# The head of a gated-linear-attention stage moved among the last projection products, its branch moved behind it

## The chip, the cores and the metric

One core of a Trainium2 chip runs the kernel. The metric is device time in microseconds: the median of three runs is 2146.17 us (2144.84 to 2146.43).

## What is computed

A decoder trunk with two layers takes 2048 prompt rows and 64 sample rows of width 1024. The first layer (pooling and differential attention) is not touched here. The second layer is gated linear attention:

```python
q, k, v, g = split(x @ w_in); log_a = log_sigmoid((x @ w_ga) @ w_gb + b_g) / 16
o, s_end = gla_chunked(q, k, v, log_a, s0)          # 4 heads, key 128, value 256
o = rms_norm(o, norm_w) * silu(g)
y = layer_norm(alpha * x + o @ w_out)
```

The recurrence works on tiles of 128 rows: o of a tile is q times the state S before it plus a causal product inside the tile, and S is carried on with the gates' decay.

## The kernel before

`project_odd` (L1426) makes q, k, gates, v and silu(g) times the norm weights. It is a Strassen-like scheme: `fast` (L184) runs seven products m in the order 1, 2, 6, 7, 4, 5, 3, each of four parts j, and yields after each part of a product's second half. Results go to DRAM: q1, k1, cb1 (gates), v1, sg1 (silu rows). Weights of a product are loaded in units of 512 KB into a ring of two raw buffers (`O.raw`, tiles wr, gs, gmi) by SP's queue, split into a hi part (L40 on ACT or L44 on DVE) and a lo part (L45 on DVE), and kept in four places (tiles wk); every fp32 product is three matmuls of such parts (L51 to L53).

In `Odd.run` (L1348) the last projection (row half 1, the gates' columns) is consumed part by part. At part (7, 3) it opens the Gla object and from then on takes one step of `early` (L1381) after each part: loads for tiles 0 and 1, the inside products of both (`inside`, L1759), splits of tile 0, and output weight 0. Then the projection's pools are closed, output weights 1 and 2 are loaded, the register `r` is read (whether the decay is too steep for the short form), and a branch runs `G.run(True)` or, in the other arm, `weights_inside` and `G.run(False)`.

`run_in` (L1816) is the tile loop. It opens its pools over the memory that the projection's tiles had (a tile waits until the old ones in its memory are no longer read), loads the sg1 rows of tiles 0 and 1 and the norm weights, and for i = 0..15 weaves `out(i - 1)` (transposes, 48 products with the output weights, LayerNorm) with `fill(i)`: `mix(i)` (o in PSUM tile go, then the state products gsp, then S, Sh, Sl), `scale(i)` (the RMS norm and gates, tile gm), three steps of the samples, and `prepare(i + 1)`. In `fill(0)` stand also output weights 3 to 7, through the same two raw buffers (tiles gs). The tile that holds o is two PSUM banks with one buffer.

The order on an engine is not the text's alone: the framework (`schedule_with_timeline_sim=True`, L2390; "the planner" below) takes the instructions that are ready by its own estimates, and the older one first. What stands in a branch is planned on its own.

Of the kernel before, what the change touches and what calls it, by code (L numbers as in the profile page):

```python
# [1312 lines left out]
class Odd:  # L1313
# [34 lines left out]
    def run(self):  # L1348
        tc, d, ctx = self.tc, self.d, self.ctx
        nc = tc.nc  # L1350
        self.steep = self.pool(ctx, "p1s", 1).tile([1, 32], I32, name="steep")[:, 0:1]
        cst = self.pool(self.p1, "p1c", 1)
        tu = self.pool(self.p1, "p1t", 4)
        last = project_odd(tc, d, self, cst, tu)
# [12 lines left out]
        self.fill_banks.close()  # L1367
        for k in range(1, 3):
            self.out_weights(G, k, self.place)
        gw = places(self.pool(ctx, "gw", 3, side="right"))  # L1370
        for k in range(3, 8):
            G.w.append((gw if k > 4 else self.place)(300 + k))
        G.buf["s"] = [self.raw.tile([128, 1024], F32, tag="raw", name=f"gs_{i}") for i in range(2)]
        r = nc.values_load(self.steep[0:1, 0:1], min_val=0, max_val=1)
        with tc.If(r < 1) as c:
            G.run(True)
        with c.Else():
# [3 lines left out]
    def early(self, G, gw):  # L1381
# [3 lines left out]

        for i in range(2):
            G.load(i, G.first + ("v1",))
        yield
        for i in range(2):
            for _ in G.inside(i, 1, True, bank):  # L1390
                yield
            if i:
                G.two("v", G.R[0], "v1", "act")
            else:
                G.two("a", G.R[0], "att", "dve")
                self.out_weights(G, 0, places(gw))
# [29 lines left out]
def project_odd(tc, d, O, cst, tu):  # L1426
# [5 lines left out]
    left = [Room(O.pool(O.p1, f"p1l{i}", 1)) for i in range(3)]  # L1432
# [280 lines left out]
class Gla:  # L1713
# [3 lines left out]
    def __init__(self, tc, d, ident, raw, gl):  # L1717
# [8 lines left out]
        for key, n, w in (("a", 1, 512), ("k", 2, 512), ("v", 1, 1024)):  # L1726
            for part in "hl":
                self.buf[key + part] = [gl.tile([128, w], F32R, name=f"g{key}{part}_{i}") for i in range(n)]
        self.buf["dec"] = [gl.tile([128, 2, 4, 8], F32, name=f"gdec{i}") for i in range(2)]
# [14 lines left out]
    def load(self, i, keys):  # L1744
# [3 lines left out]
        for key in keys:  # L1748
# [6 lines left out]
            else:  # L1755
                r[key] = self.get(key) if key == "v1" else self.io.tile([128, 1024], F32, tag=key, name=f"g{key}{i}")[:n]
# [52 lines left out]
    def run(self, fast):  # L1809

        R, buf = {i: dict(r) for i, r in self.R.items()}, {k: list(b) for k, b in self.buf.items()}
        with ExitStack() as ctx:
            self.run_in(ctx, fast)
        self.R, self.buf = R, buf

    def run_in(self, ctx, fast):  # L1816
# [8 lines left out]
        io = self.io = pool("gio", 2)  # L1825
        wk = pool("gwk", 1)
        sk = pool("gsk", 1)
        sm = pool("gsm", 4)
# [3 lines left out]
        pz = pool("gpz", 2, space=PSUM)  # L1832

        def bank(name):
            return pt.tile([128, 512], F32, tag="pt", name=name)

        first = self.first if fast else self.first + ("att",)
        S = wk.tile([128, 4, 256], F32, name="S")
        Sh = wk.tile([128, 4, 256], F32R, name="Sh")
        Sl = wk.tile([128, 4, 256], F32R, name="Sl")  # L1840
        for i in range(2):
            load(i, ("sg1",) if fast else ("att", "sg1"))
        g = wk.tile([128, 1024], F32, name="lng1")
        b = wk.tile([128, 1024], F32, name="lnb1")
        nc.sync.dma_start(g, d["ln_g"][1])
# [567 lines left out]
```

## Time and profile before

| | |
|---|---|
| median of three runs | 2146.17 us |
| the profiled execution | 2143.98 us |
| its span, first to last instruction | 2142.2 us |
| mean granted TensorE clock, of full speed | 0.978 |
| busy: PE, DVE, ACT, POOL | 94%, 69%, 48%, 41% |

PE is TensorE, DVE VectorE, ACT ScalarE, POOL GpSimd, SPq the queue of SyncE that issues most loads. In a table by stretch each engine has its busy time and its number of instructions; PEclk is the share of full speed that was granted (1.00 is 2.4 GHz, 0.50 is 1.2 GHz). In a list of instructions the first number is the start, the second the duration; in brackets stands how long the engine had been idle before it, and what ended that. Ends of matmuls are modelled.

### The profile page before, as it was taken

The page shows a single profiled execution, that of the slowest core. Times are in us where ns is not written, and L with a number is a line of the kernel's source. Part 1 is how long each engine was busy: PE and PEld are TensorE (multiplying, and loading weights), DVE is VectorE, ACT ScalarE, POOL GpSimd, SP SyncE. Part 2 cuts the span into 40 slices and gives each one's busy share as a digit, 9 for nine tenths or more (in the row PEclk, how much of TensorE's full clock was granted, in tenths as well). Part 3 has the DMA queues.
Part 4 walks back from the last instruction along what each step waited for, and adds up shares of the span by engine and source line. Part 5 has one row for each costly group of instructions (what it writes and reads, how often), then busy time and mean ns, then how long its engine had stood idle before and what let it go on. Part 6 is the DMA issues. An engine that isn't in the chain of part 4 may idle for free.

```text
span 2142.2 us, 31455 instructions
## 1 busy us (share of the span) xinstructions
PE 2007.9 (94%) x10769; PEld 1639.6 (77%) x10769; DVE 1479.3 (69%) x2762; ACT 1024.7 (48%) x1922; POOL 878.4 (41%) x1167
## 2 busy tenths in 40 slices
PE   8989998998999999889898899999999897999997
PEld 7868786877788777677786688788887676787786
DVE  7697657565876676798767776667634557777784
ACT  4144433345633455664555533445428665455552
POOL 2345444323754532666543513222111122555654
PEclk9999999999999999999999999999999998999999
DMA  8877777447964698553322558666543457455532
GB/s 289 268 247 237 254 258 233 166 110 199 285 202 150 172 293 290 157 188 121 111 70 74 175 176 301 224 215 216 167 149 126 152 180 260 148 183 179 166 107 76
DMA packets 210395, 405.64 MB, mean 189 GB/s; under 512 B 29122, under 2 KB 106306, under 8 KB 210226
## 3 DMA queue, kind: packets, MB, share of 16 engines
q1 hardware_dynamic: 139490, 231.43, 35.7%
q0 software_dynamic: 50240, 158.48, 20.9%
q10 hardware_dynamic: 20496, 13.63, 2.1%
q8 instruction: 87, 1.43, 0.3%
q14 instruction: 82, 0.67, 0.1%
HBM read 275.90 MB, written 127.55 MB: 188 GB/s over the span
## 4 chain that ended last, share of the span: by engine, by line
PE 68%; DVE 10%; DMA 9%; ACT 5%; issue 5%; POOL 2%; SPq 1%; ACTq 0%; POOLq 0%; DVEq 0%
PE f L51 11%; PE f L52 11%; PE f L53 11%; PE po L1061 3%; PE gz L53 3%; PE gz L51 3%; PE gz L52 3%; PE sc L1016 2%; PE sc L1017 2%; PE tp L1068 2%; ACT e L1036 2%; DVE nm L1021 2%; DMA pt<-pn 1%; PE zp L51 1%; PE zp L53 1%
## 5 line engine op out<-in xcount | busy, mean ns | idle before, releaser
L1036 ACT ACTIVATE e<-sc,nm 128x896 f32<-128x896 f32 (+11 forms) x192 | 164.8, 864 | 127.1 <-DVE nm L1034 89.4
L1021 DVE TENSOR_REDUCE nm<-sc 128x1 f32<-128x768 f32 (+7 forms) x160 | 156.7, 991 | 26.1 <-PE sc L1017 15.4
L45 DVE TENSOR_TENSOR wk<-wr,wk 128x1024 fp32r<-128x1024 f32 x80 | 98.3, 1230 | 97.8 <-ACT wk L40 97.6
L45 DVE TENSOR_TENSOR wl<-wr,wh 128x1024 fp32r<-128x1024 f32 (+1 forms) x90 | 108.8, 1211 | 82.1 <-ACT wh L40 72.4
L1016 PE MATMUL sc<-kst,qh 128*128 128x512 f32 (+9 forms) x352 | 134.5, 385 | 30.2 <-ACT e L1036 28.8
L1061 PE MATMUL po<-vt,aT 128*128 128x128 f32 x1088 | 154.4, 282 | 2.5 <-ACT aT L1073 2.2
L40 ACT ACTIVATE wh<-wr 128x1024 fp32r<-128x1024 f32 (+1 forms) x85 | 88.0, 1038 | 139.6 <-PE f L52 71.7
L1061 PEld LDWEIGHTS po<-vt,aT 128*128 128x128 f32 x1088 | 139.2, 196 | 9.3 <-ACT aT L1073 2.5
L40 ACT ACTIVATE wk<-wr 128x1024 fp32r<-128x1024 f32 x77 | 81.3, 1058 | 129.5 <-PE f L53 94.0
L1073 ACT ACTIVATE aT<-tp 128x512 f32<-128x512 f32 (+3 forms) x160 | 85.4, 534 | 98.0 <-PE tp L1068 97.5
L1017 PE MATMUL sc<-kst,ql 128*128 128x512 f32 (+9 forms) x352 | 122.2, 350 | 0.0
L1016 PEld LDWEIGHTS sc<-kst,qh 128*128 128x128 f32 x352 | 68.5, 195 | 50.2 <-ACT e L1036 41.0
L1068 PE MATMUL tp<-ident,e 128*128 128x128 f32 x544 | 91.2, 282 | 11.6 <-ACT aT L1073 10.2
L1045 DVE SCALAR_TENSOR_TENSOR e<-e,c,e 128x128 f32<-128x128 f32 (+15 forms) x64 | 96.1, 1502 | 1.4
L1068 PEld LDWEIGHTS tp<-ident,e 128*128 128x128 f32 x544 | 63.9, 144 | 25.8 <-ACT aT L1073 15.2
L1017 PEld LDWEIGHTS sc<-kst,ql 128*128 128x128 f32 x352 | 68.7, 195 | 4.0 <-issue 0.2
L1039 DVE TENSOR_TENSOR s<-s 128x1 f32<-128x1 f32 x64 | 21.2, 331 | 70.5 <-ACT e L1036 70.1
L1092 POOL TENSOR_SCALAR s1q<-s 128x1 f32<-128x1 f32 x64 | 16.9, 265 | 102.4 <-DVE s L1039 78.2
L53 PE MATMUL op<-wh,ol 128*128 128x512 f32 x128 | 52.7, 411 | 5.1 <-DVE ol L1232 5.1
L51 PE MATMUL op<-wh,oh 128*128 128x512 f32 x128 | 53.4, 417 | 1.2 <-ACT oh L1231 1.1
L52 PE MATMUL gz<-wl,gmh 128*128 128x512 f32 x128 | 51.5, 402 | 1.1 <-DVE wl L45 1.1
L51 PE MATMUL zp<-wh,zh 128*128 128x512 f32 x128 | 52.2, 410 | 0.0
(872 smaller groups left out, 6665.0 us busy)
## 6 DMA issues: line engine op xcount, KB each, us to landing
wr<-in_w_q SPq DMA_DIRECT2D x75, 512.0 KB, 4.9
wr<-pt SPq DMA_DIRECT2D x40, 512.0 KB, 7.5
wr<-rt SPq DMA_DIRECT2D x40, 512.0 KB, 4.4
sk<-in_cachek SPq DMA_DIRECT2D x64, 256.0 KB, 3.6
sv<-in_cachev SPq DMA_DIRECT2D x64, 256.0 KB, 4.7
pt<-pn POOLq DMA_DIRECT2D x32, 256.0 KB, 7.1
qr<-q SPq DMA_DIRECT2D x64, 128.0 KB, 4.4
kr<-k SPq DMA_DIRECT2D x32, 256.0 KB, 4.5
```

Source lines behind the costliest of these rows:

```text
L40: h = nc.scalar.activation(hi, raw, AF.Copy)
L45: return h, (lo_eng or nc.vector).tensor_tensor(out=lo, in0=raw, in1=hi, op=ALU.subtract)
L51: nc.tensor.matmul(ps, lh(k), rh(k), start=(first and k == 0), stop=False, **kw)
L52: nc.tensor.matmul(ps, lh(k), rl(k), start=False, stop=False, **kw)
L53: nc.tensor.matmul(ps, ll(k), rh(k), start=False, stop=(last and k == n - 1), **kw)
L1016: nc.tensor.matmul(o, qh[:, c, qs], kst[:, ks], start=True, stop=False)
L1017: nc.tensor.matmul(o, ql[:, c, qs], kst[:, ks], start=False, stop=k < npc - 1)
L1021: nc.vector.tensor_reduce(out=nm[:, c, i:i + 1], in_=p[:, :, :w], op=ALU.max, axis=AX.XY, negate=True)
L1036: nc.scalar.activation(o, p, AF.Exp, bias=nm[:, m, 0:1], accum_out=s[:, m, i if npc > 1 else 0:][:, :1])
L1045: nc.vector.scalar_tensor_tensor(out=es[0][:, :nk], in0=es[1][:, :nk], scalar=c2, in1=es[0][:, :nk], op0=ALU.mult, op1=ALU.add)
L1061: nc.tensor.matmul(po, s[:, 128 * j:128 * j + 128], vt[:, k0 + j, :], start=(k0 + j == 0), stop=(k0 + j == n - 1))
L1068: nc.tensor.transpose(p[:, 128 * j:128 * j + 128], a[:, 128 * (k0 + j):128 * (k0 + j) + 128], self.ident)
```

## The change

- `S`, `Sh`, `Sl` become tiles of the Gla object, in memory of their own, and not of the tile loop's pool.
- `mix` becomes a method, and o is written to two tiles of one bank each; tile 0's `mix` runs in `early`, with its o in the projection's PSUM pool.
- `early` has twelve steps and not seven: output weights 0 and 1 after both tiles' inside products, into the room of a22; tile 0's mix after part (5, 3); the splits of tile 1 and the loads of tile 2; weights 2 and 3 into the room of s1. Weights 4 to 7 go into the places wk, in `fill(0)`. All hi parts are on ACT, the lo parts of weights 3, 5 and 7 on POOL.
- The tile loop's pools are put in another order over the projection's memory: the sg1 rows lie where the tiles t were, y0 where u was, the split q and gm where v was. In `fill(0)` the loads of the samples and of the norm weights come after weights 4 to 7.
- `G.run(True)` runs without a condition, and only the other form stands in a branch, behind it.

```diff
@@ Odd.run
-                early = self.early(G, self.pool(ctx, "gw0", 1, side="right"))
+                early = self.early(G)
             elif early:
                 next(early, None)
-        for _ in early:
-            pass
+        r = nc.values_load(self.steep[0:1, 0:1], min_val=0, max_val=1)
         self.p1.close()
         self.fill_banks.close()
-        for k in range(1, 3):
-            self.out_weights(G, k, self.place)
...
-        with tc.If(r < 1) as c:
-            G.run(True)
-        with c.Else():
+        G.run(True, early)
+
+        with tc.If(r > 0):
             weights_inside(tc, d)
             G.run(False)
@@ early
+            if i == 0:
+                G.two("v", R[0], "v1", "act")
+                G.two("a", R[0], "att", "act")
+            yield
+        self.out_weights(G, 0, room(self.left[0]))
+        yield
+        self.out_weights(G, 1, room(self.left[0]))
+        yield
+        po = [self.ps.tile([128, 512], F32, tag="mm", name=f"go0_{i}").rearrange("p (j e) -> p j e", j=2)
+              for i in range(2)]
+        mix = G.mix(0, po, two)
+        for i in range(4):
+            next(mix)
+        yield
+        for _ in mix:
+            pass
+        yield
+        G.two("v", R[1], "v1", "act")
+        G.load(2, G.first + ("v1",))
+        yield
+        G.two("a", R[1], "att", "act")
+        self.out_weights(G, 2, room(self.left[1]))
+        yield
+        self.out_weights(G, 3, room(self.left[1]))
+        yield
+        for k in range(4, 8):
+            self.out_weights(G, k, self.place)
+        G.buf["s"] = [self.raw.tile([128, 1024], F32, tag="raw", name=f"gs_{i}") for i in range(2)]
@@ out_weights
-        G.w.append(Weights(self.tc, self.raw, place, 300 + k).unit(self.d["w1_out"][k]))
+        W = Weights(self.tc, self.raw, place, 300 + k)
+        W.hi_act = True
+        G.w.append(W.unit(self.d["w1_out"][k], self.tc.nc.gpsimd if k in (3, 5, 7) else None))
@@ mix
             if i == 0:
-                    nc.vector.tensor_copy(S[:, hs, :], ps)
+                nc.scalar.activation(S[:, hs, :], ps, AF.Copy)
@@ run_in
-        io = self.io = pool("gio", 2)
-        wk = pool("gwk", 1)
+        pad = pool("gpad", 1)
+        pad.tile([128, 32], F32, name="gpad")
+        wn = pool("gwn", 1)
+        wh = pool("gwh", 3)
+        self.io = {key: pool("g" + key, 2) for key in ("sg1", "y0")}
+        wq = pool("gwq", 1)
+        wl = pool("gwl", 3)
...
-        po = pool("gpo", 1, space=PSUM)
-        pst = pool("gps", 2, space=PSUM)
+        po = pool("gpo", 2, space=PSUM)
@@ fill
-            yield from mix(i)
+            if i or not fast:
+                yield from mix(i)
...
+                if fast:
+                    scale(0)
                 yield from prepare(1)
-                for k in range(3, 8):
-                    x = self.get("s")
-                    nc.sync.dma_start(x, d["w1_out"][k])
-                    split(nc, x, *w[k], "act" if k % 2 else "dve")
-                with tc.issue_after(self.split_v[0].ins), tc.issue_after(self.split_v[1].ins):
+                for _ in early or ():
+                    pass
+                load(16, first)
+                nc.sync.dma_start(g, d["ln_g"][1])
+                nc.sync.dma_start(b, d["ln_b"][1])
+                if not fast:
                     scale(0)
...
-            if i < 14:
+            if (0 if fast else -1) < i < 14:
                 load(i + 2, first + ("v1",))
```

## Rows read from the trace of the kernel before

**Rows 1.** The page's busy line: busy us, share of the span, instructions.

```profile
PE 2007.9 (94%) x10769; PEld 1639.6 (77%) x10769; DVE 1479.3 (69%) x2762; ACT 1024.7 (48%) x1922; POOL 878.4 (41%) x1167
```

**Rows 2.** Busy time by stretch, all engines; the first line names the columns.

```profile
core 0: us, PE busy (x) PEld busy (x) DVE busy (x) ACT busy (x) POOL busy (x), PEclk, DMA share, GB/s
1748.00:1754.00 6.00, 3.09 (x18) 2.28 (x17) 5.08 (x8) 5.97 (x13) 2.58 (x4) 1.00 0.66 253
...
1764.80:1779.40 14.60, 14.60 (x66) 12.03 (x65) 11.31 (x17) 5.15 (x8) 3.28 (x6) 1.00 0.24 86
...
1782.40:1789.60 7.20, 0.02 (x1) 0.01 (x1) 2.30 (x5) 4.76 (x12) 0.75 (x5) 0.67 0.96 319
1789.60:1798.60 9.00, 7.15 (x28) 5.91 (x29) 8.88 (x29) 3.16 (x6) 3.00 (x4) 0.50 1.11 349
1798.60:1822.40 23.80, 22.09 (x147) 17.95 (x146) 20.94 (x37) 17.07 (x38) 6.92 (x5) 1.00 0.90 296
1822.40:1826.40 4.00, 1.18 (x6) 0.61 (x4) 4.00 (x6) 1.60 (x3) 1.27 (x1) 0.93 0.87 255
1826.40:1832.00 5.60, 5.56 (x20) 3.78 (x21) 2.98 (x12) 2.67 (x9) 1.17 (x2) 0.50 0.47 141
...
1900.00:2000.00 100.00, 100.00 (x567) 79.53 (x566) 77.47 (x169) 54.47 (x124) 54.52 (x42) 1.00 0.58 185
```

**Rows 3.** PE's waits, 1745 to 2143: us in total, times, longest.

```profile
PE gsp L51 <- DVE S L1891: 7.8, 2, 7.2
PE gso L1952 <- DMA gs<-in_state_gla: 2.9, 1, 2.9
PE f L51 <- ACT wk L40: 2.9, 1, 2.9
PE gsp L51 <- ACT gvh L40: 2.3, 1, 2.3
```

**Rows 4.** PE's instructions in order of time, 1764 to 1830.

```profile
1764.79 3.88 PE L273 MATMUL ycy<-wk,ys 128*128 128x512 f32 x16
...
1779.39 0.28 PE L51 MATMUL go<-gvh,gah 128*128 128x256 f32 x1
...
1782.14 0.28 PE L53 MATMUL gsp<-gvh,gkl 128*128 128x256 f32 x1
1789.62 0.55 PE L51 MATMUL gsp<-gvh,gkh 128*128 128x256 f32 x1 [7.20 <-DVE S L1891]
```

**Rows 5.** DVE's instructions in order of time, the first one after the stop.

```profile
1788.18 0.69 DVE L45 TENSOR_TENSOR Sl<-gsp,Sh 128x512 fp32r<-128x512 f32 x1 [4.90 <-DMA sg<-u]
```

**Rows 6.** The chain of waits, 1650 to 1830: start, us, what.

```profile
1781.97 6.10 DMA sg<-u
```

**Rows 7.** SP's queue in order of time, 1735 to 1830.

```profile
1736.43 0.33 SPq L375 DMA_DIRECT2D wr<-in_w_out  x1
...
1742.09 1.45 SPq L375 DMA_DIRECT2D wr<-rt  x2
1753.25 3.00 SPq L375 DMA_DIRECT2D wr<-in_w_q  x2
...
1781.70 0.83 SPq L1757 DMA_DIRECT2D gsg<-sg  x2
...
1822.08 0.35 SPq L1944 DMA_DIRECT2D gs<-in_state_gla  x1
```

**Rows 8.** Line 375's loads, 1700 to 1830, from issue to landing.

```profile
DMA to landing us min/median/max: 7.9/8.3/8.6
```

**Rows 9.** ACT's and DVE's instructions on the last product's weights.

```profile
1757.09 1.06 ACT L40 ACTIVATE wk<-wr 128x1024 fp32r<-128x1024 f32 x1 [1.26 <-DMA wr<-in_w_q]
...
1760.87 1.23 DVE L45 TENSOR_TENSOR wk<-wr,wk 128x1024 fp32r<-128x1024 f32 x1 [1.46 <-ACT wk L40]
```

**Rows 10.** POOL and DVE in order of time, from 2006.

```profile
2006.08 2.81 POOL L1304 TENSOR_TENSOR gy<-gy,lnb 128x1024 f32<-128x1024 f32 x1
2006.65 2.80 DVE L45 TENSOR_TENSOR Sl<-S,Sh 128x512 fp32r<-128x512 f32 x1
```

More of the change, by code (lines that the diff above doesn't have):

```diff
@@ L1351, in run @@
         self.steep = self.pool(ctx, "p1s", 1).tile([1, 32], I32, name="steep")[:, 0:1]
+        self.left = [Room(self.pool(ctx, f"p1l{i}", 1)) for i in range(2)]
         cst = self.pool(self.p1, "p1c", 1)
         tu = self.pool(self.p1, "p1t", 4)
+        self.left.append(Room(self.pool(self.p1, "p1l2", 1)))
         last = project_odd(tc, d, self, cst, tu)
@@ L1389, in early @@
         for i in range(2):
[L1390 to L1396, printed above, removed]
-            yield
+            inside = G.inside(i, 1, True, bank)
+            next(inside)
+            yield
+            for _ in inside:
+                pass
[27 more added lines that the diff above has]
+        G.buf["s"] = [self.raw.tile([128, 1024], F32, tag="raw", name=f"gs_{i}") for i in range(2)]
     def out_weights(self, G, k, place):
-        G.w.append(Weights(self.tc, self.raw, place, 300 + k).unit(self.d["w1_out"][k]))
+        W = Weights(self.tc, self.raw, place, 300 + k)
+        W.hi_act = True
+        G.w.append(W.unit(self.d["w1_out"][k], self.tc.nc.gpsimd if k in (3, 5, 7) else None))
 def plain_rows(X, nc, w, bank, sink):
@@ L1431, in project_odd @@
     W.hi_act = True
-    left = [Room(O.pool(O.p1, f"p1l{i}", 1)) for i in range(3)]
+    left = O.left
     later = []
@@ L1830, in run_in, with mix @@
-        pst = pool("gps", 2, space=PSUM)
+        po = pool("gpo", 2, space=PSUM)
         pt = pool("gpt", 2, space=PSUM)
         pz = pool("gpz", 2, space=PSUM)
+        pst = pool("gps", 2, space=PSUM)
         def bank(name):
             return pt.tile([128, 512], F32, tag="pt", name=name)
+        def mix(i):
+            return self.mix(i, [po.tile([128, 2, 256], F32, tag="po", name=f"go{i}_{z}") for z in range(2)],
+                            lambda name: pst.tile([128, 2, 256], F32, tag="ps", name=name))
@@ L1837, in run_in @@
         first = self.first if fast else self.first + ("att",)
-        S = wk.tile([128, 4, 256], F32, name="S")
-        Sh = wk.tile([128, 4, 256], F32R, name="Sh")
-        Sl = wk.tile([128, 4, 256], F32R, name="Sl")
         for i in range(2):
[L1842 to L1845, printed above, removed]
-        nc.sync.dma_start(b, d["ln_b"][1])
+            load(i, ("sg1",) if fast else first + ("v1", "sg1"))
@@ L1848, in prepare @@
+        g = wn.tile([128, 1024], F32, name="lng1")
+        b = wn.tile([128, 1024], F32, name="lnb1")
         def prepare(i):
             r = R[i]
-            if i > 1:
+            ready = fast and i < 2
+            if not ready:
                 yield from self.inside(i, 1, fast, bank)
-            if i:
-                self.split_v = self.two("v", r, "v1", "act")
-            if i or not fast:
+                self.two("v", r, "v1", "act")
                 self.two("a", r, "att", "act")
@@ L2025, in out @@
             ln.finish(d["y1"][t0:t0 + n, :], i == 15)
-        load(16, first)
-        side = samples(R[16])
+        side = samples(R.setdefault(16, {}))
         for _ in prepare(0):
@@ L2036, in fill @@
             else:
+                if fast:
+                    scale(0)
                 yield from prepare(1)
-                for k in range(3, 8):
-                    x = self.get("s")
-                    nc.sync.dma_start(x, d["w1_out"][k])
-                    split(nc, x, *w[k], "act" if k % 2 else "dve")
-                with tc.issue_after(self.split_v[0].ins), tc.issue_after(self.split_v[1].ins):
+                for _ in early or ():
+                    pass
+                load(16, first)
+                nc.sync.dma_start(g, d["ln_g"][1])
+                nc.sync.dma_start(b, d["ln_b"][1])
+                if not fast:
                     scale(0)
```

114 lines of the change are left out of this document (60 added, 54 removed).

## The prediction

> **What bounds the kernel now.** I read the busy line first: TensorE (PE) is busy for 94% of the span [rows 1]. So the time is PE's work plus the places where PE stands or runs at the lower clock, and a change that takes no matmul away is worth what it takes of those. Next the stretches [rows 2]: from 1900 to 2000 us PE is busy all the time at clock 1.00, so whatever is gained or lost before reaches the end undiminished. The bad part is 1748 to 1832, the change from the last projection product to the tile loop. The list of PE's waits names the stops [rows 3]: 7.8 us for the copy of S (L1891), 2.9 us for a product's weights (L40), 2.9 us for a sample's state, and one of 2.3 us far behind, near 2017.
>
> The 7.2 us stop is followed back through three views. PE's last tile-0 matmul starts at 1782.14 and its next one at 1789.62 [rows 4]. What it waits for is a PSUM bank that VectorE (DVE) empties with the subtraction into Sl and the copy into S; DVE starts the first of these at 1788.18, after 4.90 us in which it waited for a DMA named sg<-u [rows 5]; the two copies of S stand behind it on DVE. The chain of waits shows that DMA: 6.10 us from 1781.97 [rows 6]. So it is a wait for memory, not for data: S, Sh and Sl lie where the last product's results (tiles u) are still being written out to sg1. Two granted clocks follow: 0.50 in the 9.0 us after the stop [rows 2], and again 0.50 in 1826.4 to 1832 after the stop of 2.8 us.
>
> **The change, part by part.** All durations are of the profiled execution: span 2142.2 us, its own time 2143.98. The median of the three runs is 2146.17, 2.2 us more; I add that at the end.
>
> *A. S, Sh, Sl in memory of their own; tile 0's mix among the products; o in two banks.* The wait for sg<-u has no object left. Idle taken away: 7.2 us in 1782.4 to 1789.6 and 9.00 - 7.15 = 1.85 us in the next stretch [rows 2]. Of that stretch's 7.15 us of matmuls at clock 0.50, half, 3.6 us, goes when the clock stays at 1.00. Together 12.6 us. Tile 0's 24 matmuls (first 1779.39, last 1782.14, so 2.9 us [rows 4]) only move ahead of the product's end; PE does them either way. What is late next: tile 1's 36 matmuls can go at once, 36 x 0.12 = 4.3 us, because its splits are now made during the products and its two o banks are those of the last product's results, free one addition after it. Bounds: 7.2 us (the stop alone goes, what follows stays scattered) to 12.6. I take 12.6, as each of the follow-up waits hangs on the DVE and ACT work that piled up during the stop.
>
> *B. Output weights 0 and 1 behind the fifth product's weights, not the first ahead of them.* In before, the load of output weight 0 goes out at 1736.43, then eight loads for tiles 0 and 1, and only at 1742.09 the two loads of product 5 [rows 7]; they take 8.3 us to land [rows 8], and PE stops 2.9 us [rows 3]. With weight 0 behind them, a raw buffer is free for them at 1736.4. Bounds 0 to 2.9 us; I take 2.9, since an issue at 1736.4 plus 8.3 is 1744.7, ahead of the last PE work before the stop.
>
> *C. Output weights 2 to 7 earlier, the state's load earlier.* In before the raw ring passes weights 3 to 7 on after 1788, and the sample's state is issued at 1822.08 [rows 7]. Idle in 1798.6 to 1822.4 and 1822.4 to 1826.4: 1.7 + 2.8 us; half of 5.56 us at clock 0.50 after it: 2.8 us [rows 2]. Bounds 0 to 7.3. I take 3.7, half: four weights are still behind the product's end, and the state's loads still stand behind them in the ring.
>
> *D. New: output weights 0 and 1 ahead of the last product's weights in the two-buffer raw ring.* One pass of a unit through the ring is a landing plus 1.06 us on ACT plus 1.23 us on DVE [rows 9]. The landing was at most 3.8 us for the last product's weights (issue 1753.25 [rows 7], split from 1757.09 [rows 9]) and 8.3 for product 5's [rows 8], so a pass is 6.1 to 10.6 us. Before, the second unit was ready at 1760.87 + 1.23 = 1762.1 and first used at 1764.79 [rows 4]. After, PE wants it at about the same time (2.9 us earlier by B, 2.9 later by tile 0's matmuls). One pass later, with product 5's loads up to 5.7 us earlier (1742.09 - 1736.43), the units are ready between 1762.5 and 1772.7. Stop: 0 to 8 us. I take 2: the nearest row is that of the same weights, with the short landing. Behind the waiting instruction on PE stands the whole last product, so nothing covers it.
>
> What such a stop does to the clock the rows leave open: after 2.85 us of standing at 1749 the stretch kept 1.00, after 2.8 us at 1823 it fell to 0.50 [rows 2]. The Trainium skill ("TensorE: Matmul & The Clock Gate", Part 1, the HAM clock gate) says that the low rate is the default and that activity lifts it; if every new stop were followed by the low rate, a price like that of 1826 to 1832, 2.8 us, would come on top of D. The sum does not use it.
>
> *E. Tile 0's products in the middle of the last product.* Their four accumulations go through the two banks that the samples' product also uses, and ACT and DVE must empty these between their other work. The trace of before has no such place; the nearest row is the 1.85 us of idle, in pieces, where PE goes hand in hand with DVE from 1789.6 to 1798.6 [rows 2]. Bounds 0 to 1.9, at either of two places, so 0 to 3.7; I take 1, half of one.
>
> *F. Weights 4 to 7 behind y0's load.* The first y0 tile now lies where the last product's first results are, so SP's queue stands at that load until they are written, and weights 4 to 7 may stand behind it; the sg1 rows of tiles 0 and 1 no longer do: in before their load waited till 1781.70 [rows 7]. A pass of 6.1 to 10.6 us each for two pairs puts the last weights 12 to 21 us after y0's load. PE meanwhile has 4.3 us of tile 1 and 5.8 us of products with weights 0 to 3 (24 x 0.24, the pace of the 16 matmuls from 1764.79 [rows 4]), and the planner may take loads ahead. Bounds 0 (12 less 10, with tile 2's products to fill it) to 11 (21 less 10); I take 2, nearer the low end, because half of those loads find their ring buffers free before the product ends.
>
> *Edits at nothing:* the hi halves of all output weights on ACT (three more of them, 1.06 us each [rows 9]; ACT is busy for 5.15 of 14.6 us in the last product [rows 2]; without that cover 3 us); the branch behind the fast version (an equal jump over the other one was there before; 0 to 1 us); three lo halves on POOL instead of DVE. For the last, the row is: a DVE subtraction with both inputs in SBUF took 2.80 us beside a POOL instruction of 2.81 us [rows 10], against 0.69 for the one that reads PSUM [rows 5]. So three POOL instructions of 2.8 us could hold DVE for 8.4 us where 3 x 1.23 = 3.7 are saved. DVE's idle 3.3 us in the last product [rows 2] covers one of them; if none is covered it is 4.7 us of DVE, not of PE. The Trainium skill ("SBUF — State Buffer", Who interferes with whom) says that the second of two such instructions waits for the whole of the first; by it this edit works against the change, by the rows DVE still has room.
>
> Sum: -12.6 - 2.9 - 3.7 + 2 + 1 + 2 = -14.2 us. 2143.98 - 14.2 = 2129.8; plus 2.2 is **2132**.
>
> **The rivals.**
>
> *1. The last product starves (slower).* Place: PE ahead of the samples' matmuls at 1764.79. The ring puts two output weights between product 5's and the last product's; if product 5's loads go out no earlier than now and all landings are the long ones, the stop is up to 8 us by D, another pass of 10.6 if the planner also puts a third output weight ahead, and the clock is halved afterwards (3.6 us as in A): 22 us against the 12.6 + 3.7 of A and C, B being lost and E and F left at nothing. 2146.2 + 6 = 2152. It decides from a stop of about 13 us, which with the clock costs what A and C bring. For it: two buffers only, 8.3 us landings, DMA engines near full. Against it: DMA share was 0.24 during the last product [rows 2], so landings there should be short.
>
> *2. The stop moves (no change).* The wait for sg<-u ends and PE meets the next late transfer: DMA share is 0.90 to 1.11 from 1782 to 1822 [rows 2]. If weights 4 to 7 come at F's upper bound (11 us), B and C give nothing, and the clock stays as it is, -12.6 + 11 = -1.6: 2144.6. The change then also would not do what it says, if the planner, which orders instructions itself, leaves tile 0's products behind the last one. Against it: much of the traffic (output weights 0 to 3, tile 2, sg1) moves ahead to where the DMA share is 0.24.
>
> *3. All stops go (more gain).* A, B and all of C, no D to F: 12.6 + 2.9 + 7.3 = 22.8, 2123; if the stop near 2017 goes too, since a half of o comes free earlier, 2.3 us and its clock more: about 2119. For it: most of what PE waited for is now done a product earlier.
>
> **How the numbers follow.** Forecast 0.55 (2125 to 2140), all stops gone 0.15, no change 0.15, starved 0.15. A measurement of this kernel tells about 0.2%, 4.3 us, from no change. Faster by more than that takes the first two, 0.70; same 0.15; slower 0.15. The range reaches from rival 3 with the stop of 2017 left (2121) to near rival 1 (2150).
>
> **What would show it.** Right: no DVE wait for sg<-u; S written by ACT; tile 0's go and gsp matmuls ahead of the last f matmul; clock 1.00 from there through tile 1; SP's w_out loads 4 to 7 out before the product's end or shortly behind. Wrong: a PE stop ahead of the samples' matmuls (D), or among the first gz matmuls (F), or POOL subtractions beside stretched DVE ones on the chain. A stop of over 13 us before the last product would turn the forecast round.

## The result, and the profile after

The changed kernel is slower: 2157.79 us median of 8 runs (2147.15 to 2161.95) against 2146.30 of 8 runs of before, ratio 1.0044 [1.0025, 1.0063], by the ratio some 9 us more where the prediction had 14 less. The profiled execution took 2149.34 us (span 2147.4, clock 0.980), at the lower end of its runs; it has 5 of those 9 us, and they can be placed.

Runs of one kernel differ by several us, and their mean granted clock lies between 0.973 and 0.983 for either kernel. Two more measures help, and the tables below use them. *At full speed* is the mean over a kernel's timed runs of span times mean granted clock; for before it is 2095 to 2096 in each of the five groups of runs, while the mean time of these groups goes from 2146.0 to 2148.7. Single runs scatter by some 3 us in it too, so that a mean of 12 is good to about 1 us. *By work* cuts the profiled execution where the same amount of TensorE work is left (columns streamed by the 10769 matmuls, as time at 2.4 GHz): from 300 to 280 us left is the stretch with the stop for a product's weights, from 280 to 240 the change to the tile loop, from 240 to 12 the loop; in before these begin at 1738, 1765 and 1832 us.

```
us by work      300-280  280-240  240-12   at full speed, timed runs
before             26.2     67.0   287.9   2095 to 2096
after              23.1     69.4   291.0   2106
after - before     -3.1     +2.4    +3.1    +10
```

So the stop at 1749 went, the change to the loop became no shorter, and the loop, which the prediction had costed at nothing, became longer. (The last 12 us of work took 2.2 us more in after, and 0.6 us had been lost before 1738.)

PE's waits after, from 1745 us on, as [rows 3]:

```profile
engine line waited for: us in total, times, longest us
PE gap L1829 <- DVE gm L1946: 11.5, 1, 11.5
PE go L52 <- DVE Sl L45: 2.8, 2, 2.2
PE gsp L51 <- DVE S L1869: 2.6, 2, 2.1
PE gsp L51 <- ACT gvh L40: 2.0, 2, 1.5
...
PE f L51 <- ACT wk L40: 1.7, 1, 1.7
PE gsp L51 <- ACT S L1875: 1.0, 1, 1.0
```

The 7.2 us stop is gone, and so is that for a sample's state. A new one of 11.5 us stands there: the scores of the 64 sample rows (gap) wait for the bank that held half of tile 0's o, until tile 0's norm (gm) has read it. The busy time by stretch shows what that does, as [rows 2]:

```profile
core 0: us, PE busy (x) PEld busy (x) DVE busy (x) ACT busy (x) POOL busy (x), PEclk, DMA share, GB/s
1762.00:1780.00 18.00, 16.34 (x83) 13.71 (x82) 13.94 (x19) 13.27 (x19) 6.02 (x7) 1.00 0.73 236
1780.00:1790.00 10.00, 5.35 (x19) 3.69 (x18) 9.98 (x18) 8.06 (x18) 6.65 (x9) 0.73 0.75 239
1790.00:1800.00 10.00, 1.50 (x7) 0.94 (x6) 4.70 (x15) 4.62 (x6) 6.69 (x5) 0.50 0.96 333
1800.00:1810.00 10.00, 7.00 (x44) 6.75 (x48) 4.92 (x11) 5.47 (x14) 1.28 (x1) 0.58 0.86 277
1810.00:1820.00 10.00, 9.79 (x62) 6.93 (x61) 7.73 (x19) 4.97 (x13) 1.02 (x1) 1.00 0.39 109
1820.00:1832.00 12.00, 12.00 (x76) 10.46 (x75) 6.54 (x14) 6.48 (x18) 4.46 (x5) 1.00 0.38 108
```

PE stands 4.65 + 8.50 + 3.00 + 0.21 = 16.4 us from 1780 to 1820; in before it was 7.18 + 1.85 + 1.71 + 2.82 = 13.6 from 1782.4 to 1826.4 [rows 2]. From 1790 to 1800 no engine is full, and everything waits for something else; the DMA engines are nearly full (0.96, 333 GB/s). The chain of waits says for what (pieces under 0.2 us left out):

```profile
1783.49 3.52 POOL wk L45
1787.03 4.28 DMA wr<-in_w_out
1791.39 1.06 ACT wk L40
...
1792.53 2.35 POOL wk L45
1794.90 0.33 SPq L1982
...
1795.32 5.84 DMA gsg<-sg
1801.29 1.67 DVE gm L1946 x4
1803.00 1.13 PE gap L1829 x8
```

The rows of sg1 that tile 0's norm needs are the last link. SP's queue shows why they are so late:

```profile
1787.03 0.33 SPq L375 DMA_DIRECT2D wr<-in_w_out  x1
1789.22 0.46 SPq L1956 DMA_DIRECT2D gs<-v  x1
...
1794.90 0.33 SPq L1982 DMA_DIRECT2D gs<-in_state_gla  x1
1795.32 0.85 SPq L1790 DMA_DIRECT2D gsg<-sg  x2
```

They go out at 1795.32 (before: 1781.70 [rows 7]), behind the last output weight, the samples' v and a sample's state. The first and the last of these load into the two raw buffers and wait there for a split: the weight for POOL's lo half, 3.52 us, the state for the last one, that ends at 1794.88. ACT and DVE stand in the same places:

```profile
1791.39 1.06 ACT L40 ACTIVATE wk<-wr 128x1024 fp32r<-128x1024 f32 x1 [2.63 <-DMA wr<-in_w_out]
```

```profile
1801.29 1.66 DVE L1946 SCALAR_TENSOR_TENSOR gm<-go,rmofg,gsg 128x256 f32<-128x256 f32 x4 [2.32 <-DMA gsg<-sg]
```

In the loop the stop for Sl, the lo part of S, near 2026 is the largest that grew; in before the same wait took 0.75 us.

```profile
2026.30 0.39 PE L52 MATMUL go<-Sl,gqh 128*128 128x256 f32 x1 [2.18 <-DVE Sl L45]
```

### The profile page after: what moved, and what is told of

Same layout as the page of the kernel before. It is cut to its first block, busy times and chain, and to the rows that moved or that the text cites. A ratio compares the mean times of both kernels' runs of the same rounds, so it can differ in the third digit from the quotient of the medians.

```text
span 2147.4 us, 31463 instructions
## 1 busy us (share of the span) xinstructions
PE 2005.4 (93%) x10769; PEld 1633.9 (76%) x10769; DVE 1478.0 (69%) x2753; ACT 1029.1 (48%) x1930; POOL 884.4 (41%) x1170
## 4 chain that ended last, share of the span: by engine, by line
PE 59%; DVE 12%; DMA 12%; issue 7%; ACT 6%; POOL 4%; SPq 1%; ACTq 0%; POOLq 0%; DVEq 0%
PE f L51 9%; PE f L52 9%; PE f L53 9%; PE po L1061 3%; PE gz L51 2%; PE gz L52 2%; PE gz L53 2%; PE sc L1016 2%; PE sc L1017 2%; PE tp L1068 2%; DMA wr<-pt 2%; DVE nm L1021 2%; ACT e L1036 2%; PE zp L51 1%; PE zp L53 1%
## 5 line engine op out<-in xcount | busy, mean ns | idle before, releaser
L40 ACT ACTIVATE wk<-wr 128x1024 fp32r<-128x1024 f32 x84 | 88.5, 1056 | 135.7 <-PE f L53 87.3
L51 PE MATMUL gz<-wk,gmh 128*128 128x512 f32 x256 | 103.4, 404 | 0.9 <-ACT gmh L40 0.7
L52 PE MATMUL gz<-wk,gmh 128*128 128x512 f32 x256 | 102.2, 399 | 0.0
L53 PE MATMUL gz<-wk,gml 128*128 128x512 f32 x256 | 101.5, 399 | 0.0
L1017 PEld LDWEIGHTS sc<-kst,ql 128*128 128x128 f32 x352 | 68.1, 193 | 4.1 <-issue 0.2
L51 PEld LDWEIGHTS gz<-wk,gmh 128*128 128x128 f32 x256 | 48.6, 190 | 12.1 <-ACT gmh L40 1.7
```

Of the source, the lines that this page charges most:

```text
L40: h = nc.scalar.activation(hi, raw, AF.Copy)
L51: nc.tensor.matmul(ps, lh(k), rh(k), start=(first and k == 0), stop=False, **kw)
L52: nc.tensor.matmul(ps, lh(k), rl(k), start=False, stop=False, **kw)
L53: nc.tensor.matmul(ps, ll(k), rh(k), start=False, stop=(last and k == n - 1), **kw)
L1017: nc.tensor.matmul(o, ql[:, c, qs], kst[:, ks], start=False, stop=k < npc - 1)
```

## The experiments

The first theory was the chain above: the rows of sg1, late on SP, hold a PSUM bank. The rival was that the bank's place alone makes the stop. As stop after stop moved, the question became which of all that is late is late last, and what the halves of o do in the loop by themselves. Each group of runs has runs of before on the same chip. All results first:

```
                      ratio to before [95%]    300-280 280-240 240-12  full speed - before
e1_banks_swapped      1.0045 [1.0026, 1.0063]   23.1    71.6   291.0   +10.7
e2_gates_rows_early   1.0021 [1.0003, 1.0040]   23.1    67.5   291.6    +6.3
e3_both               1.0031 [1.0016, 1.0045]   23.2    70.1   290.0    +5.6
e4_own_memory_alone   1.0007 [0.9991, 1.0022]   28.8    68.6   288.0    +3.9
e5_banks_apart        1.0059 [1.0042, 1.0076]   23.1    73.3   289.4    +7.3
e6_banks_and_rows     1.0041 [1.0027, 1.0054]   23.3    68.2   292.3   +10.4
e7_and_act_order      1.0035 [1.0018, 1.0052]   23.5    70.9   290.5    +7.9
e8_o_halves_alone     1.0024 [1.0008, 1.0040]   30.2    62.3   293.2    +6.8
e9_o_whole_again      1.0009 [0.9997, 1.0021]   23.1    70.6   287.0    +4.5
e10_low_halves_on_dve 1.0037 [1.0021, 1.0054]   23.1    72.0   293.2   +10.6
e11_all_mended_halves 1.0043 [1.0025, 1.0061]   23.1    71.4   293.2    +8.0
e12_all_mended_o_whole 1.0019 [1.0001, 1.0038]  23.1    70.7   287.4    +5.5
e13_y0_off_u          1.0007 [0.9992, 1.0021]   23.1    68.1   288.8    +2.7
e14_act_behind_split  1.0013 [1.0000, 1.0026]   23.1    66.2   288.7    +1.1
e15_four_loads_less   0.9991 [0.9973, 1.0009]   23.1    62.3   286.7    +1.2
e16_s_and_q_off_u     1.0010 [0.9993, 1.0028]   29.5    64.8   286.1    +0.8
e17_and_weight_behind 1.0013 [0.9997, 1.0029]   23.1    66.3   293.1    +3.8
e18_tile0_in_run      1.0036 [1.0020, 1.0051]   23.1    68.2   286.7    +5.0
```

The columns by work come from one execution each; the others from 7 to 12 timed ones. How far one execution can be trusted: in the loop before, e4 and e16 have the same order of matmuls and take 287.9, 288.0 and 286.1 us; from 300 to 280 the kernels that leave the stop for a product's weights as it was (before, e4, e8, e16) take 26.2 to 30.2.

**The bank, the rows, and what stands behind them.** e1 exchanges the pools of `bank` and of the output products, over the projection's PSUM:

```diff
-        pt = pool("gpt", 2, space=PSUM)
         pz = pool("gpz", 2, space=PSUM)
+        pt = pool("gpt", 2, space=PSUM)
```

> The changed kernel with the two PSUM pools of the loop exchanged, so that the samples' products (gkp, gap) no longer take the banks of tile 0's o. The gates' rows still go out last on SP. Theory 1 (the gates' rows are late, and the samples' product, queued ahead of tile 1's o, waits for the bank that gm reads): gap starts by 1793 us, tile 1's matmuls follow at once, the stop of 11.5 us shrinks to under 2, but a new stop of 2 to 8 us stands ahead of tile 0's transposes gmt, since gm still begins at about 1801; 4 to 9 us faster than the changed kernel. Rival (ACT, DVE and POOL are overfull at the end of the last product, whatever PE's order): less than 2 us faster. Second rival (what is lost lies outside the transition): no difference.

A miss: tile 0's o lies on two banks, one in each pool's place, and the exchange put the other one into the way, for the product gkp:

```profile
1805.79 1.03 PE L1810 MATMUL gkp<-ident,gf 128*64 128x128 f32 x4 [13.66 <-DVE gm L1946]
```

e2 takes the pool of the sg1 rows from the tiles t to memory that is free earlier (here and below, ... stands for lines left out):

```diff
-        self.io = {key: pool("g" + key, 2) for key in ("sg1", "y0")}
+        self.io = {"y0": pool("gy0", 2)}
...
-        sk = pool("gsk", 1)
         wj = pool("gwj", 1)
+        self.io["sg1"] = pool("gsg1", 2)
+        sk = pool("gsk", 1)
```

> The changed kernel with the gates' rows (sg1) in the memory of the last product's wide parts, which is free long before, where they lay on tiles t; their two loads then stand on SP ahead of the samples' rows, the layer norm's rows and the sample state instead of behind them. Banks as in the changed kernel. Theory 1: the loads go out near 1782 us and land by 1788, gm begins by 1793, gap by 1795; the stop of 11.5 us falls to 2 to 4 us and the clock is back earlier; 7 to 11 us faster than the changed kernel. Rival (engines overfull at the product's end): DVE is busy anyway, gm begins no earlier than 1797, at most 4 us faster. Second rival: no difference.

The rows went out at 1789.16, in an execution that reaches 280 us of work left 7.5 us later than after's, so 13.7 us earlier than there; yet the stop shrank from 11.5 to 10.0 us only. Its end now was the norm itself, whose squares stood on ACT behind the last output weight. e3 has both edits:

> The changed kernel with both edits: PSUM pools exchanged, and the gates' rows in the wide parts' memory. Theory 1: no stop over 3 us between 1780 and 1830; 9 to 13 us faster than the changed kernel, that is 0 to 5 us under the kernel before by the profiled runs (2143.98 and 2149.34). Rival (engines overfull at the product's end): at most 4 us faster than the changed kernel. Second rival: no difference.

The stop stayed, 11.7 us, and ACT says what is late:

```profile
1792.30 1.06 ACT L40 ACTIVATE wk<-wr 128x1024 fp32r<-128x1024 f32 x1 [7.63 <-DMA wr<-in_w_out]
```

ACT stood 7.63 us at the hi half of the last output weight, whose load went out at 1784.68, when POOL's 3.50 us lo half ended; behind it on ACT stood the squares and tile 1's queries. e5 puts both banks of tile 0's o out of the way of the samples' products (a pool of one bank on each side of the output products'):

```diff
-        pt = pool("gpt", 2, space=PSUM)
+        pt = [pool("gpt0", 1, space=PSUM)]
         pz = pool("gpz", 2, space=PSUM)
+        pt.append(pool("gpt1", 1, space=PSUM))
```

> The changed kernel with the pool of the samples' products (gkp, gap) split in two one-bank pools on both sides of pz, so that neither lies on a bank of tile 0's o; e1 had only moved the wait from gap to gkp. Gates' rows late as in the changed kernel. Theory 1 (PE stands because the samples' product waits for the bank that gm reads): gap runs by 1793 us without a wait; tile 1's o then waits only for its own split gqh on ACT, which stands behind the last output weight and the samples' v (1791 to 1795), and PE has 7 us of work until gmt has to wait for gm (1803 to 1808): stops of 2 to 4 us and 3 to 5 us take the place of the one of 11.5; 2 to 5 us faster than the changed kernel. Theory 2 (what decides is ACT's queue: the hi half of the last output weight waits 5 to 8 us for its load ahead of tile 0's squares and tile 1's split): at most 2 us faster. Rival (the loop behind, not the transition, holds the loss): no difference from the changed kernel, and the stretch from 1830 us to the end is as long as there.

e6 adds e2's edit to it:

> As e5, and the gates' rows early as in e2. Theory 1: no stop over 4 us is left between the product's end and 1830; 6 to 10 us faster than the changed kernel. Theory 2 (ACT's queue behind the last output weight): squares, gm and gqh still come 6 to 8 us behind the weight's load, one stop of 6 us or more is left; at most 4 us faster than the changed kernel. Rival (the loop behind): no difference.

e7 also holds the last weight's and the samples' v's hi halves on ACT until the squares and the queries have gone:

```diff
-        for k in range(4, 8):
+        for k in range(4, 7):
             self.out_weights(G, k, self.place)
+        with self.tc.issue_after(G.sq.ins), self.tc.issue_after(G.hold.ins):
+            self.out_weights(G, 7, self.place)
...
```

> As e6, and on ACT the hi halves of the last output weight and of the samples' v are held behind tile 0's squares and tile 1's split gqh. Theory 2: the squares run at about 1785 us, gm by 1791, tile 1's products follow the samples' at once; no stop over 3 us; 8 to 13 us faster than the changed kernel and 4 us or more faster than e6. Theory 1: as e6 within 2 us. Rival (the loop behind): no difference; by the profiles, the stretch from 1830 us on would then still be some 3 us longer than before.

The bank was the stop's place, not its cause: in e5 it is gone, and PE stands for tile 1's queries (2.5 and 2.2 us) and for the output products' gm (4.1) in its stead. In e6 and e7 it is the queries too (4.6, 3.8), in e7 because ACT waited 8.30 us for sg<-u at their split: e2's order of pools had moved them onto u.

**S alone.** e4 is before with S, Sh, Sl in memory of their own and nothing else, e16 takes tile 1's split queries off u as well, e17 puts output weight 0 behind the inside products (part B):

```diff
+        sp = self.pool(ctx, "gS", 1, side="right")
+        G.S = sp.tile([128, 4, 256], F32, name="S")
...
-                r["qs"] = tuple(wk.tile([128, 4, 128], F32R, tag=f"q{z}", name=f"gq{z}{i}") for z in "hl")
+                r["qs"] = tuple(self.wq.tile([128, 4, 128], F32R, tag=f"q{z}", name=f"gq{z}{i}") for z in "hl")
...
-                self.out_weights(G, 0, places(gw))
             yield
+        self.out_weights(G, 0, places(gw))
+        yield
```

> The kernel before with one part of the change: S, Sh and Sl in memory of their own, free before the last product ends; all else as before, tile 0's products behind the last product. The prediction's part A by its lower bound: the stop of 7.2 us on sg<-u goes, 7 to 12 us faster than before. Theory 1 (something late stands right behind it): PE goes on with tile 0 and then meets the gates' rows, whose load still goes out at about 1782 us, and the output weights; 2 to 6 us faster. Rival (the stop only moves): within 2 us of the kernel before.

> The kernel before with S, Sh, Sl and also tile 1's split queries in memory of their own; all else as before. In e4, with S alone moved, ACT stood 7.6 us at the split queries, which lay on tiles u as well. The prediction's part A (7.2 to 12.6 us for the stop): the transition takes 81 to 87 us where the kernel before took 93.1 and e4 97.4; 7 us or more faster than before. Theory 3 (the next thing on tiles u shows: here SP stands at the layer norm's rows, with the samples' rows, y0 and four weights behind it): 0 to 4 us shorter, within 0.2% of before.

> As e16, and output weight 0 behind the fifth product's weights (the prediction's part B): the stop of 2.9 us near 1749 goes. Part B: 2.9 us faster than e16. Theory 3: the same for B, since that stop stands alone; 1 to 5 us faster than before in all. Rival: output weight 0 then comes later, and the last product or the transition gives it back, no faster than e16.

In e4 DVE no longer waits for sg<-u; ACT does, at the next tile that lies on u (tile 1's split queries), and PE stands 9.6 us behind ACT:

```profile
1788.43 0.63 ACT L40 ACTIVATE gqh<-ge 128x512 fp32r<-128x512 f32 x1 [7.57 <-DMA sg<-u]
```

In e16 S is copied at 1783.56, five us earlier than in before. But the wait for sg<-u has only moved once more: ACT now stands at it for the scratch tile gj of tile 0's squares, and DVE stands behind ACT. On DVE the next update of S comes behind that and behind the samples' gates, whose rows land later still:

```profile
1788.49 0.38 ACT L1906 ACTIVATE gj<-go 128x256 bf16<-128x256 f32 x1 [4.65 <-DMA sg<-u]
```

```profile
1783.56 0.68 DVE L1894 COPY S<-gsp 128x512 f32<-128x512 f32 x1
...
1790.52 0.17 DVE L2295 TENSOR_SCALAR rmofg<-gss 128x4 f32<-128x4 f32 x1 [3.91 <-ACT gj L1906]
1792.28 0.43 DVE L1773 TENSOR_TENSOR gf<-gcb 128x256 f32<-128x256 f32 x1 [1.59 <-DMA gcb<-cb]
...
1793.40 0.38 DVE L1888 SCALAR_TENSOR_TENSOR S<-S,gdec,gsp 128x256 f32<-128x256 f32 x1
```

```profile
1793.84 0.58 PE L51 MATMUL gsp<-gvh,gkh 128*128 128x256 f32 x1 [5.99 <-DVE S L1888]
```

In before the rows of these gates were as late, and the same matmul started at the same time:

```profile
1791.94 0.42 ACT L1766 ACTIVATE ge<-gcb 128x256 f32<-128x256 f32 x1 [4.67 <-DMA gcb<-cb]
```

```profile
1793.57 0.58 PE L51 MATMUL gsp<-gvh,gkh 128*128 128x256 f32 x1 [0.49 <-DVE S L1885]
```

So the stop of 7.2 us became one of 6.0 us a little further on, and by 1793 us nothing was gained, where the prediction had 7.2 to 12.6. By work the change to the loop took 64.8 us, 2.2 less than in before; but PE's idle time in it is 13.9 us against 13.6, and what differs is the granted clock of that one execution (0.895 against 0.856 in this stretch). The timed runs show no gain: 1.0010 [0.9993, 1.0028]. No kernel here takes every tile off u and leaves all else as in before. e17 has part B's gain besides (23.1), and a loop that the planner ordered otherwise, 293.1 us, with o whole.

**o in halves.** e8 is before with o in two one-bank halves from two buffers, e9 is after with o in one two-bank tile from tile 1 on (its edit is shown):

```diff
-        po = pool("gpo", 2, space=PSUM)
+        po = pool("gpo", 1, space=PSUM)
...
-            return self.mix(i, [po.tile([128, 2, 256], F32, tag="po", name=f"go{i}_{z}") for z in range(2)],
+            p = po.tile([128, 4, 256], F32, tag="po", name=f"go{i}")
+            return self.mix(i, [p[:, 0:2, :], p[:, 2:4, :]],
```

> The kernel before with o in two one-bank halves alone; all else as before. From the profiles, the loop behind the transition takes 315 to 316.5 us in the changed kernel and e1 to e3 for the same PE work that takes 310.7 in the kernel before and 312.7 in e4. If the halves (and the order that the planner makes of them) cause it: the loop takes 315 us or more, and the kernel is 2 to 4 us slower than before. If the cause lies elsewhere in the loop's memory or order: within 1.5 us of before. The prediction's third rival (the stop near 2017 goes): 2 to 3 us faster than before.

> The changed kernel with the halves of o undone: from tile 1 on, o is again one tile of two banks. If the halves cost what e8 showed (2150.9 against 2146.5, and a loop of 318 us for work that took 311 to 313 with o whole): the loop from 1830 us on is 3 us or more shorter than in the changed kernel, and the kernel is 3 to 6 us faster than it (ratio to before 1.0015 to 1.003 where the changed kernel had 1.0044). If the loop's loss comes from the rest of the change: no difference from the changed kernel.

The halves alone cost 0.24% [0.08, 0.40]; without them after is 1.0009 [0.9997, 1.0021], no change. In e9 the stop of the transition is still there (12.6 us), so the two are apart. PE's stops in e8's loop, from 2010 to 2055 us:

```profile
2018.60 0.39 PE L52 MATMUL go<-gvl,gah 128*128 128x256 f32 x1 [0.39 <-DVE gvl L45]
2025.09 0.50 PE L51 MATMUL gsp<-gvh,gkh 128*128 128x256 f32 x2 [1.53 <-ACT gvh L40]
2032.31 0.39 PE L52 MATMUL go<-Sl,gqh 128*128 128x256 f32 x1 [3.00 <-DVE Sl L45]
```

As one half's bank is free earlier, the planner puts the next tile's o products on PE earlier (the one that waits stands at 90.7 us of work left, in before at 89.5), and there they stand at the lo part of S, which DVE has not made yet. PE's idle time in the loop was 5.6 us in before and 9.9 in e8, but 6.9 in e9 and 7.7 in after: 4.3 of the 5 us that the halves cost by e8's ratio, and only 0.8 of the 4.0 by work between e9 and after. The rest is time in which PE counts as busy; what makes it slower there, the profiles don't show.

**The lo halves on POOL.** e10 puts the three of them back on DVE:

```diff
-        G.w.append(W.unit(self.d["w1_out"][k], self.tc.nc.gpsimd if k in (3, 5, 7) else None))
+        G.w.append(W.unit(self.d["w1_out"][k]))
```

> The changed kernel with the low halves of output weights 3, 5 and 7 on DVE again, not on POOL. The chain that ended last in the changed kernel passes through three POOL subtractions (2.4, 3.5 and 2.35 us) that free the ring for the last weight's load. Theory 2 (ring and ACT's queue): the last weight's load goes out 2 to 4 us earlier, the 11.5 us stop shrinks by as much; 2 to 5 us faster than the changed kernel. Rival (the prediction's price of nothing): within 1.5 us of it. Second rival (DVE is full in 1780 to 1790): 1 to 3 us slower.

1.0037 against 1.0044: no difference that shows, though POOL's 3.52 us stands in after's chain. The stop was 13.9 us.

**Everything mended, one after the other.** e11 has e7's edits, the lo halves on DVE and the queries on the tiles t; e12 has o whole besides:

> All that was found in the transition mended together, o still in halves: banks apart, gates' rows early, ACT's order as in e7, low halves on DVE, and tile 1's split queries on memory of tiles t, where e2, e3, e6 and e7 had them on tiles u, so that they waited for the last product's write-out (8.3 us on ACT in e7, as in e4). Theory 2: tile 1's o follows within 2 us of the samples' product, no stop over 3 us in 1785 to 1815; the transition is 5 to 10 us shorter than in the changed kernel; 5 to 10 us faster than it. Rival (the sum of ACT's and DVE's work and of the loads sets the transition, whatever the order): at most 3 us faster, with the stops only spread.

> As e11, and o whole again. If both causes hold and add: 3 to 5 us faster than e11, 8 to 14 us faster than the changed kernel, that is 0 to 5 us faster than the kernel before. If the transition is set by the sum of work: as e9 within 3 us.

Again halves against whole: 293.2 against 287.4 us of loop, 1.0043 against 1.0019. The transition was no shorter than after's. PE stood 4.2 us for the split of gm, which stood on ACT behind tile 3's gates:

```profile
1811.20 0.63 ACT L1802 ACTIVATE ge<-gcb 128x512 f32<-128x512 f32 x1 [5.99 <-DMA gcb<-cb]
```

and these rows were late because SP had stood at y0's load, whose tile lies on u. e13 moves y0 off u, e14 also holds tile 3's gates on ACT behind tile 0's split gm, e15 also leaves the loads of weights 4 to 7 out and splits weight 3's rows for them, 2 MB less:

```diff
+        pool("gpad2", 1).tile([128, 512], F32, name="gpad2")
+        self.io = {"y0": pool("gy0", 2)}
```

```diff
...
+            if fast and i == 3:
+                after.enter_context(self.tc.issue_after(self.gmh.ins))
+            nc.scalar.activation(e, r["cb1"], AF.Exp, scale=1.0 / 16)
```

```diff
...
+        G.w.append(place(301 + k))
+        split(self.tc.nc, self.w3, *G.w[k], "act")
```

> As e12, with the rows y0 on memory of tiles v and not of tiles u. In e12 SP stood at y0's load until the last product's write-out ended (1800.8 us), and the sample state and tile 3's rows went out only behind it; ACT then stood 6.0 us for tile 3's rows ahead of tile 0's transposed split, PE 4.2 us for that and 2.5 us for the state. Theory 3 (the transition is a chain of transfers: whichever row is loaded last holds an engine's queue, and mending one shows the next): y0 out by 1797, state and tile 3's rows 3 to 5 us earlier, the transition 3 to 5 us shorter; 3 to 5 us faster than e12. Theory 4 (the transfers' sum sets the transition, DMA share 0.9 to 1.0): no shorter than e12 by more than 1.5 us, with other rows late.

> As e13, and tile 3's first Exp on ACT is held behind tile 0's transposed splits. Theory 3: the 4.2 us stop ahead of gz goes, gz starts by 1808 us where e12 had 1813.4; another 2 to 5 us faster than e13. Theory 4: gz starts earlier but then waits for weights or rows; within 1.5 us of e13.

> As e14, with output weights 4 to 7 split from weight 3's rows; their four loads (2 MB) are left out, all engine work stays. Theory 4 (transfers set the transition): the transition is 6 us or more shorter than in e14, since 2 MB at 340 GB/s are 6 us. Theory 3: 2 to 5 us shorter, as only the rows behind the last weight's load come earlier. Rival (ACT's and DVE's own work and hand-offs set it): within 1.5 us of e14.

By work 70.7, 68.1, 66.2 and 62.3 us: each step shortens the transition by 2 to 4 us (the 1.9 from e13 to e14 are no more than one order of matmuls differed by in the loop), and what is left in e14 is five stops of 1.6 to 3.4 us with five different causes:

```profile
PE gso L2004 <- DMA gs<-in_state_gla: 3.4, 1, 3.4
PE gsp L51 <- DVE S L1875: 3.3, 1, 3.3
PE go L53 <- DVE gql L45: 2.4, 1, 2.4
PE f L51 <- ACT wk L40: 1.7, 1, 1.7
PE gsp L51 <- ACT S L1881: 1.6, 1, 1.6
```

In the timed runs e13 and e14 are level with before, e15 too (0.9991 [0.9973, 1.0009]), so even without those loads the transition gives at most 0.3%. The 3.9 us by work that 2 MB less bring are what a chain of waits was expected to give back (2 to 5), not the 6 or more of transfers whose sum sets the pace.

**Tile 0's place.** e18 is e9 with tile 0's mix back in the loop, behind the products; tile 0 then uses the split v of tile 1:

```diff
-        mix = G.mix(0, po, two)
-        for i in range(4):
-            next(mix)
...
-            if i or not fast:
-                yield from mix(i)
+            yield from mix(i)
```

> As e9 (the changed kernel with o whole), and tile 0's products behind the last product again, not among its matmuls; by the planner's order the samples' product then stands behind them on a bank that tile 0's o does not hold. If tile 0 among the products is worth what the prediction had (A less E, some 11 us): slower than e9 by 4 us or more. Theory 3 (the transition is paced by rows and hand-offs, not by PE's order): within 2.5 us of e9.

1.0036 [1.0020, 1.0051] against e9's 1.0009: by the ratios tile 0's place among the products is worth some 6 us. The profile (68.2 against 70.6 by work) and the time at full speed (+5.0 against +4.5) don't show that, so it stays open.

No version beat before by more than its interval.

## Why the prediction was wrong, step by step

- **A (-12.6), the step that failed.** In after the wait for sg<-u is gone as forecast, and S is written by ACT. But the step let the whole stop go, and the clock with it, because the chain showed that wait last; "tile 1's 36 matmuls can go at once" was only argued. What is late next was late by nearly as much: tile 1's queries on the same memory (e4), the squares' scratch tile there and the samples' gates (e16), the sg1 rows (after), the last output weight ahead of the squares on ACT (e3), y0 on SP (e12). The samples' gates could be read in before: their rows end ACT's wait at 1791.94, 3.8 us after the wait for sg<-u. The lower bound, 7.2, was not a bound: the row of the stop says how long the named wait lasted, not how long PE would stand without it. By their intervals e4 and e16 are at most 0.09% and 0.07% faster than before, under 2 us; what the wait would be worth with every tile off u stays open.
- **F (+2).** That "the sg1 rows of tiles 0 and 1 no longer" stand behind a wait was wrong. The new pool lies on the tiles t, and both rows' loads were issued only at 1795.32, 13.6 us later than before, behind all the output weights and a sample's state on SP. That the planner gives the pool free as a whole, when its last tile has been written out, fits the order of the issues but was not tried.
- **C (-3.7).** The stop for the state and the clock behind it did go: clock 1.00 from 1810 to 1832. It bought nothing that shows; that the same work stood in the stop ahead of it instead is argued, not tried. A and C to F together were forecast at -11.3 and measured +2.4 by work, in one execution.
- **B (-2.9)** was right: 23.1 against 26.2 us, -3.1, and 23.1 to 23.5 in every kernel that has it; the ones without it have 26.2 to 30.2.
- **D (+2)** was right: 1.66 us at 1765.60. The prediction left open what such a stop does to the clock: 1762 to 1780 kept 1.00. In after the clock fell to 0.50 at 1784.6, behind stops of 0.5 and 1.0 us and ahead of the long one, stayed there through it, and rose at 1808.5, when PE had worked without a stop from 1803. The rule of the Trainium skill ("TensorE: Matmul & The Clock Gate", Part 1, the HAM clock gate) that the prediction named there is that the low rate is the default and activity lifts it; the rise at 1808.5 agrees.
- **E (+1)** was taken for the wrong place. The two banks of tile 0's o did no harm among the products; they held up the samples' scores, behind the products' end (after, e1).
- **Edits at nothing.** The lo halves on POOL: right in sum (e10). Beside POOL's subtractions of 2.40 and 3.51 us a 64x512 DVE subtraction (yco) took 2.23 us where e10 has 0.68, and a small DVE copy 1.13 where e10 has 0.16; and the POOL one of 3.51, where the others took 2.34 and 2.40, stood beside a DVE subtraction of 1.21 us that began, by these rough POOL spans, 0.07 us behind it. The Trainium skill ("SBUF — State Buffer", Who interferes with whom) says that the second waits for the whole of the first; the two DVE instructions that grew agree, and for the third pair 0.07 us is too little to say which was first. The hi halves on ACT were not at nothing: in e3 the 7.63 us that ACT stood at one of them (2.63 in after) held up all behind it.
- **The loop, not in the sum.** Halves of o stood in the prediction only as a gain (rival 3, "since a half of o comes free earlier"). They were its largest loss: 0.24% added (e8), 0.35% taken away again (1.0044 to 1.0009), 0.24% in e11 against e12, so 5 to 7.5 us. All ten kernels with halves have 289.4 to 293.2 us of loop by work; of the ten with o whole nine have 286.1 to 288.8, and only e17 has 293.1.
- **The rivals.** Rival 2, the stop moves, was the mechanism of the transition, though not for the price of F's upper bound: PE never waited for the weights 4 to 7. Its -1.6 us (2144.6) is near what after without the halves shows, +1.9 us [-0.6, +4.5] (e9). Rival 1 did not happen (1.66 us, where it wanted 13). Rival 3's sums do not meet: with the stop of 2017 left they give 2123, not the 2121 of the range. No rival had the loop.

So the account is: -3.1 (B) and +2.4 (the rest of the transition) instead of -14.2, and the halves on top. After's profiled execution adds up by work, 5.2 us in all; where the rest of the timed runs' 9 to 10 us lies, this one profile does not show.

## What to carry to other kernels

Where many queues run into a change of stage, the wait that the chain shows last is one of several that end close together: price its removal by the end of the second latest (in before: 1791.94 against 1788.18), found by listing for each engine and each DMA queue what stands at its head in that window, not by the length of the stop. When a tile's pool is moved, look up what lay in each new place and when its last reader is done, for loads as well as for tiles. A PSUM tile that comes free earlier is not a gain in itself where a planner fills PE in order: it may put ahead what then waits for another engine.

## What was not expected of the hardware

The same kernel's runs differ by up to 20 us (before: 2137.75 to 2157.64) with the granted clock at 0.973 to 0.982, while span times clock is 2095 to 2096 on average in five groups of runs; for differences of 0.2% the profile of a single execution is too little. And a stop's label can name the wrong engine: in e3 the profile gives POOL's ge as what ended the 11.7 us, where by the matmul's bank (e1 has the same wait) it was DVE's gm; the two end within 0.1 us of each other.
